# Token-row projections of an encoder block: 512 columns of w_in per matmul instead of 256

## The chip, the cores and the metric

The kernel runs on one core of one Trainium2 chip. The core has five engines that each work through their own instructions in order and wait for one another by semaphores: TensorE (matmuls, PE in the profile, with its weight loads as PEld), VectorE (DVE), ScalarE (ACT), GpSimd (POOL) and SyncE (SP), which here issues nearly all DMAs. The metric is the device time of one execution in microseconds, lower is better.

## What is computed

The reference is one layer of an encoder block on 1024 tokens of 1024 channels, in float32: an input norm with a modulation, two token mixers on the same normed input `h` (bidirectional retention with 4 heads of 128, differential attention with 4 heads), a gated merge, an output projection, and 16 expert feed-forwards of which each takes 128 tokens. What matters here is the projection of `h` and what its columns are used for:

```
h = _rmsnorm(x, norm_mix_g[l]) * (1.0 + sc1) + sh1
proj = h @ w_in[l]
rq, rk, rv, rg, dq1, dq2, dk1, dk2, dvv, gr, gd = jnp.split(proj, split_points, axis=-1)
rq = _rotate(rq.reshape(B, S, RET_HEADS, RET_DK), pos)
rk = _rotate(rk.reshape(B, S, RET_HEADS, RET_DK), pos) * (RET_DK ** -0.5)
...
```

`rq`, `rk`, `rv`, `rg` (retention) and `dvv` (the values of the attention) have 512 columns each, and these five are wanted with tokens as rows. `dq1` to `dk2` and the gates `gr`, `gd` are wanted with channels as rows.

## The kernel before

**Split numbers.** A float32 product is made of three matmuls on rounded parts: every operand is kept as a high part (`hi`, rounded by ScalarE) and a low part (`lo`, the difference, by VectorE or GpSimd). `mm3` issues high x high, high x low, low x high. `hH` and `hL` hold the parts of `h`, with channels as rows, in eight pieces of 128 channels (`k`).

**Weights.** The class `Weights` walks through one list of row blocks of 128 x 1024 float32 (512 KB). The first 44 are `w_in`: blocks 0 to 7 for the attention's q and k, then five groups of four for `dvv`, `rv`, `rk`, `rq`, `rg` (called v, r_v, r_k, r_q, r_g here), then 16 for the gates. `load` issues a block's DMA on SP's queue into one of two buffers `raw`; `split_to` makes `hi` (ScalarE) and `lo` (GpSimd in this stage, as `W.eng = G`) in one of four buffer pairs (`HL = 4`); `take` hands blocks to a projection. A raw buffer is refilled after its `lo`; the refill is issued three ticks after the split (`W.lazy = 3`), and a tick passes with each step of the weave.

**Two kinds of projection.** `proj_T` makes 128 channels as rows: one block, 8 steps, moving operand `h` with 512 columns, the weights held in the array. `proj_N` makes tokens as rows: 128 tokens of `hH`/`hL` are held in the array and the weights move. In before.py one call makes 256 columns from two blocks (each block has four `k` side by side, 256 columns each), in 16 steps of 12 matmuls with 256 columns. Its sums stand in a PSUM tile `mm` [128, 2, 256] for 256 tokens, from a pool of two. When a tile is done, `finish`, which runs at the first step of the next tile, issues its evacuation: for v a split in `hi` and `lo` with two stores to `vs` (`evac_v`), for r_v and r_g a copy by ScalarE, for r_k and r_q the rotation, four VectorE operations on 256 columns (`px` x cos, `px` x sin, for two groups of tokens) and two GpSimd operations, and one store to `rs` (`evac_r`). Stores are issued two ticks later on SP's queue.

**The weave.** `weave` runs the steps of the projections (`gen_d`: five `proj_T`, then v and r_v; `gen_r`: r_k, r_q, r_g; `gen_g`: the gates) and puts steps of side work between them in a fixed proportion: first `gen_mod` (modulation rows, mostly VectorE), then `gen_attn` (107 pieces to 117 steps), then `gen_ret`. This order is the program order on every engine. A round of the attention (128 queries of one head) is: 8 score matmuls into two tiles `big`; on VectorE the bias with a maximum (`soft`); on ScalarE two exponentials; the scale of the one by ScalarE and the scale-and-add of both by VectorE (`combine`); and, in the next round, 8 transposes and the splits of the result into `at`, with 24 matmuls of probabilities times values every second round.

These lines set how many blocks are held and when the next are split:

```
HL = 4
hl2 = W.take(2, ahead=False)
if t2 < 2 and u == 1 and g == 0:
    W.split_to(W.held + 3 + t2)
```

The last two lines split, in the first and the second of four tiles, the two blocks of the next call.

Of the kernel before, what the change touches and what calls it, by code (L numbers as in the profile page):

```python
# [10 lines left out]
F32 = mybir.dt.float32  # L11
F32R = mybir.dt.float32r
# [64 lines left out]
def lay_out(w):  # L77

    w_in = np.asarray(w["w_in"])[0]
    rq, rk, rv, rg, q1, q2, k1, k2, dv, gr, gd = np.split(  # L80
        w_in, np.cumsum([512, 512, 512, 512, 256, 256, 256, 256, 512, 1024, 1024])[:-1], axis=1)

    def pair(a, b):
        return np.concatenate([a.reshape(D, 4, 1, 64), b.reshape(D, 4, 1, 64)], 2).reshape(D, 512)

    def halves(a):
        return a.reshape(D, 4, 64, 2).transpose(0, 1, 3, 2).reshape(D, 512)

    def blocks(a):
        n = a.shape[1] // 128  # L90
        return a.reshape(8, 128, n, 128).transpose(2, 1, 0, 3).reshape(n, 128, 1024)

    def wide(a):
        n = a.shape[1] // 256
        return a.reshape(2, 4, 128, n, 256).transpose(3, 0, 2, 1, 4).reshape(n * 2, 128, 1024)

    win = np.concatenate([blocks(pair(q1, q2)), blocks(pair(k1, k2)), wide(dv),
                          wide(rv), wide(halves(rk)), wide(halves(rq)), wide(rg), blocks(gr), blocks(gd)], 0)
    wr = np.asarray(w["w_ret_out"])[0].reshape(4, 128, 8, 128).transpose(2, 1, 0, 3)
    wd = np.asarray(w["w_diff_out"])[0].reshape(4, 128, 8, 128).transpose(2, 1, 0, 3)  # L100
    wout = np.concatenate([wr, wd], 2).reshape(8, 128, 1024)

    def col(v, n=8):
        return np.asarray(v).reshape(n, 128).T

    cols = np.concatenate([col(w["c"]), col(w["norm_mix_g"]), col(np.asarray(w["b_ada"])[0, 0:1024]),
                           col(np.asarray(w["b_ada"])[0, 1024:2048]), col(w["diff_subln_g"], 1),
                           col(w["norm_ffn_g"]), col(w["final_g"])], 1)
    lam = np.concatenate([np.asarray(w[n]) for n in ("lambda_q1", "lambda_k1", "lambda_q2", "lambda_k2")], 0)
    rows = np.concatenate([np.asarray(w["b_ada"])[0].reshape(6, 1024)[2:], np.asarray(w["norm_ffn_g"])], 0)  # L110
    return {
        "x": np.asarray(w["x"])[0], "w_ada": np.asarray(w["w_ada"])[0], "w_in": win, "w_out": wout,
        "w_o": np.asarray(w["w_o"])[0], "cols": cols, "lam": lam, "rows": rows,
        "gn": np.asarray(w["ret_gn_g"]), "rel_bias": np.asarray(w["rel_bias"]),
        "w_router": np.asarray(w["w_router"])[0].reshape(8, 128, 16).transpose(1, 0, 2).reshape(128, 128),
        "w_gate": np.asarray(w["w_exp_gate"])[0], "w_up": np.asarray(w["w_exp_up"])[0],
        "w_down": np.asarray(w["w_exp_down"])[0],
    }
# [3 lines left out]
def encoder_block(ctx: ExitStack, tc: tile.TileContext, a, out, lim=99, tap=None):  # L122
# [4 lines left out]
    def r32(ap):  # L127
        return ap.bitcast(F32)
# [408 lines left out]
    def finish():  # L537
        while done:
            done.pop(0)()
# [19 lines left out]

    def proj_N(evac):  # L560

        hl2 = W.take(2, ahead=False)
        for t2 in range(4):
            p = pp.tile([128, 2, 256], F32, name="mm")
            for u in range(2):
                s = slice((t2 * 2 + u) * 128, (t2 * 2 + u) * 128 + 128)
                for g in range(2):
                    if u == 0 and g == 0:
                        finish()
                    if t2 < 2 and u == 1 and g == 0:  # L570
                        W.split_to(W.held + 3 + t2)
                    for k in range(g * 4, g * 4 + 4):
                        hi, lo = hl2[g]
                        c = slice((k % 4) * 256, (k % 4) * 256 + 256)
                        mm3(p[:, u, :], hH[:, k, s], hL[:, k, s], hi[:, c], lo[:, c], k == 0, k == 7)
                    if u and g:
                        done.append(lambda p=p, t2=t2: evac(p, t2))
                    yield

    def evac_qk(i):  # L580
        f = 0.125 if i < 4 else 1.0
# [12 lines left out]
            defer(2, st)  # L594
        return go

    def evac_v(c):
        def go(p, t2):
            oh_ = evp.tile([128, 2, 256], F32R, name="ev0")
            ol_ = evp.tile([128, 2, 256], F32R, name="ev1")  # L600
            split(oh_[:], ol_[:], p[:])

            def st():
                for l, o in ((0, oh_), (1, ol_)):
                    SY.dma_start(r32(vs[l, t2 * 256:(t2 + 1) * 256, c * 256:(c + 1) * 256])
                                 .rearrange("(t p) c -> p t c", p=128), r32(o[:]))
            defer(2, st)
        return go

    tiles = {}  # L610

    def evac_r(n, c):
        def go(p, t2):
            o = evp.tile([128, 2, 256], F32, name="ev0")
            if n in "vg":
                A.activation(o[:], p[:], AF.Copy)
            else:
                f = KSCALE if n == "k" else 1.0
                t1 = evp.tile([128, 2, 2, 2, 64], F32, name="ev1")
                for u in range(2):  # L620
                    t = t2 * 2 + u
                    px = p[:, u, :].rearrange("p (h d) -> p h d", h=4)
                    cb = tiles["cst"][:, t, None, 0:64].to_broadcast([128, 4, 64])
                    sb = tiles["cst"][:, t, None, 64:128].to_broadcast([128, 4, 64])
                    V.scalar_tensor_tensor(o[:, u, :].rearrange("p (h d) -> p h d", h=4), px, f, cb,
                                           op0=OP.mult, op1=OP.mult)
                    V.scalar_tensor_tensor(t1[:, u].rearrange("p h f d -> p (h f) d"), px, f, sb,
                                           op0=OP.mult, op1=OP.mult)
                ox = o[:].rearrange("p u (h f d) -> p (u h) f d", h=2, f=2)
                tx = t1[:].rearrange("p u h f d -> p (u h) f d")  # L630
                G.tensor_tensor(ox[:, :, 0], ox[:, :, 0], tx[:, :, 1], op=OP.subtract)
                G.tensor_tensor(ox[:, :, 1], ox[:, :, 1], tx[:, :, 0], op=OP.add)
            defer(2, lambda: SY.dma_start(rs[n][t2 * 256:(t2 + 1) * 256, c * 256:(c + 1) * 256]
                                          .rearrange("(t p) c -> p t c", p=128), o[:]))
        return go

    def gen_d():
# [7 lines left out]
            defer(3 + 3 * i, lambda i=i: SY.dma_start(r32(qs[i]).rearrange("l p c -> p l c"), xT[:, 2 * i:2 * i + 2, :]))  # L645
        for i in range(3, 8):
            yield from proj_T(evac_qk(i))
        for c in range(2):
            yield from proj_N(evac_v(c))
        for c in range(2):  # L650
            yield from proj_N(evac_r("v", c))

    def gen_mod():

# [195 lines left out]

    def gen_r():
        for n in "kqg":
            for c in range(2):
                yield from proj_N(evac_r(n, c))


    rctx = ctx.enter_context(ExitStack())
# [1105 lines left out]
```

## Time and profile before

| | |
|---|---|
| median of 3 runs | 1611.27 us (1608.58 to 1614.94) |
| the profiled execution, its own time | 1607.37 us |
| its span | 1605.5 us |
| TensorE busy | 1530.6 us, 95% |
| VectorE, ScalarE, GpSimd busy | 1186.8, 886.5, 468.8 us |

The span is the time from the first to the last instruction in the trace; some 2 us of the execution lie around it. Busy time counts an engine's instructions once where they overlap. Matmuls overlap: the mean duration of one is longer than the distance to the next. The projections with tokens as rows run from about 135 to 520 us.

### The profile page before, as it was taken

How to read it: one execution, taken by the hardware profiler on the slowest of the kernel's cores; microseconds unless marked ns; L12 is line 12 of the kernel's file. 1: busy time of each engine (PE TensorE's matmuls, PEld its weight loads, DVE VectorE, ACT ScalarE, POOL GpSimd, SP SyncE). 2: the span in 40 equal slices, each digit the busy share in tenths (PEclk: the TensorE clock that was granted, in tenths of full speed). 3: DMA queues.
4: the chain of work that ended last, by engine and by line, in shares of the span. 5: the costliest groups of instructions: out<-in, count | busy, mean ns of one | idle time of the engine just before them, and what ended most of it. 6: DMA issues, size and time to landing. Idle time of an engine off the chain costs nothing. (4 is left out here: it accounts for less than half of the span.)

```text
span 1605.5 us, 23860 instructions
## 1 busy us (share of the span) xinstructions
PE 1530.6 (95%) x8493; PEld 1282.6 (80%) x8493; DVE 1186.8 (74%) x2037; ACT 886.5 (55%) x1165; POOL 468.8 (29%) x330
## 2 busy tenths in 40 slices
PE   6999999999999999999998997999999999999994
PEld 5778989989898688888877875578888888888882
DVE  6754357778772356663578866899999999999995
ACT  7712156555564444443244343477777777777874
POOL 1342212231311343443000005353433444334310
PEclk8999999999999999999999999999999999999998
DMA  9798453343423484344897687699999999999926
GB/s 315 232 358 305 146 156 113 94 119 100 137 86 105 153 302 149 129 141 145 258 355 242 201 326 267 264 386 397 390 384 392 381 375 387 390 393 386 383 94 249
DMA packets 174019, 408.91 MB, mean 255 GB/s; under 512 B 18712, under 2 KB 71576, under 8 KB 173900
## 3 DMA queue, kind: packets, MB, share of 16 engines
q1 hardware_dynamic: 161916, 368.06, 63.7%
q0 software_dynamic: 9104, 34.08, 7.3%
q10 hardware_dynamic: 2880, 5.24, 0.9%
q8 instruction: 67, 1.10, 0.3%
q14 instruction: 52, 0.43, 0.1%
HBM read 350.65 MB, written 57.73 MB: 254 GB/s over the span
## 5 line engine op out<-in xcount | busy, mean ns | idle before, releaser
L131 PE MATMUL big<-hi,xh 128*128 128x512 f32 x494 | 202.1, 409 | 1.7 <-DVE yraw L1800 1.7
L131 PE MATMUL big<-lo,xh 128*128 128x512 f32 x494 | 195.5, 396 | 0.0
L131 PE MATMUL big<-hi,xl 128*128 128x512 f32 x494 | 195.5, 396 | 0.0
L140 POOL TENSOR_TENSOR lo<-raw,hi 128x1024 fp32r<-128x1024 f32 x44 | 107.4, 2442 | 280.1 <-ACT hi L139 275.8
L140 DVE TENSOR_TENSOR lo<-eraw,hi 128x1024 fp32r<-128x1024 f32 x139 | 169.4, 1226 | 23.9 <-ACT hi L139 20.3
L131 PE MATMUL mm<-hi,hH 128*128 128x256 f32 x640 | 183.8, 287 | 0.0
L131 PE MATMUL mm<-lo,hH 128*128 128x256 f32 x640 | 180.9, 283 | 0.0
L131 PE MATMUL mm<-hi,hL 128*128 128x256 f32 x640 | 180.8, 282 | 0.0
L139 ACT ACTIVATE hi<-eraw 128x1024 fp32r<-128x1024 f32 x139 | 146.0, 1057 | 40.4 <-PE big L131 39.9
L1615 POOL TENSOR_SCALAR oh<-tab,aff 128x128 bf16<-128x128 f32 x112 | 157.1, 1426 | 2.6 <-DVE aff L1736 2.6
L131 PE MATMUL mm<-hH,hi 128*128 128x512 f32 x352 | 141.7, 402 | 3.4 <-ACT hH L415 2.3
L131 PE MATMUL mm<-hL,hi 128*128 128x512 f32 x352 | 138.1, 392 | 1.6 <-DVE hL L420 1.6
L131 PE MATMUL mm<-hH,lo 128*128 128x512 f32 x352 | 137.9, 392 | 0.0
L131 PEld LDWEIGHTS mm<-hi,hH 128*128 128x128 f32 x640 | 122.2, 191 | 4.8 <-DVE xt L678 1.7
L131 PEld LDWEIGHTS mm<-lo,hH 128*128 128x128 f32 x640 | 122.4, 191 | 1.3
L131 PEld LDWEIGHTS mm<-hi,hL 128*128 128x128 f32 x640 | 122.3, 191 | 0.0
L783 ACT ACTIVATE e<-e,m 128x1024 f32<-128x1024 f32 x64 | 73.6, 1150 | 82.8 <-DVE m L777 82.7
L131 PEld LDWEIGHTS big<-hi,xh 128*128 128x128 f32 x494 | 93.3, 189 | 23.4 <-ACT hi L139 2.1
L131 PEld LDWEIGHTS big<-hi,xl 128*128 128x128 f32 x494 | 92.9, 188 | 22.5 <-DVE xl L140 0.3
L131 PEld LDWEIGHTS big<-lo,xh 128*128 128x128 f32 x494 | 93.1, 189 | 21.1 <-issue 1.2
L139 ACT ACTIVATE hi<-raw 128x1024 fp32r<-128x1024 f32 x79 | 83.0, 1055 | 35.9 <-PE big L131 10.6
L775 DVE CUSTOM_DVE_ANT_0 e<-big,strip 128x1024 f32<-128x1024 f32 x64 | 77.8, 1216 | 30.6 <-PE big L131 30.6
(491 smaller groups left out, 3791.1 us busy)
## 6 DMA issues: line engine op xcount, KB each, us to landing
raw<-in_w_in_dram SPq DMA_DIRECT2D x43, 512.0 KB
eraw<-in_w_gate_dram SPq DMA_DIRECT2D x41, 512.0 KB
eraw<-in_w_up_dram SPq DMA_DIRECT2D x38, 512.0 KB
eraw<-in_w_down_dram SPq DMA_DIRECT2D x34, 512.0 KB
wada<-in_w_ada_dram POOLq DMA_DIRECT2D x16, 1024.0 KB, 8.5
eraw<-in_w_o_dram SPq DMA_DIRECT2D x26, 512.0 KB
mh<-in_w_gate_dram SPq DMA_DIRECT2D x17, 512.0 KB
wada<-in_w_ada_dram SPq DMA_DIRECT2D x16, 512.0 KB
```

The lines of the kernel that those rows point to most:

```text
L131: T.matmul(o, l, r, start=start, stop=stop)
L139: A.activation(hi, src, AF.Copy)
L140: eng.tensor_tensor(lo, src, r32(hi), op=OP.subtract)
L775: V.tensor_tensor_reduce(e[:], p[:], strip[:, 896 - 128 * qb:1920 - 128 * qb], scale=1.0, scalar=-3.0e38, op0=OP.add, op1=OP.max, accum_ou ...
L783: A.activation(e[:], e[:], AF.Exp, bias=m[:], accum_out=z[:])
L1615: eng.tensor_scalar(o[:, g], tab[:, C_IOTA:C_IOTA + 128], slots[e][:, g:g + 1], None, op0=OP.is_equal)
```

## The change

The host lays out the five groups of `w_in` in another way (`wide`): a block has two `k` with all 512 columns each instead of four `k` with 256. One call of `proj_N` makes all 512 columns from four blocks in 32 steps of 6 matmuls with 512 columns, for eight tiles of 128 tokens; five calls take the place of ten. The PSUM tile is [128, 512], as large as before, an evacuation has 128 tokens x 512 columns, and a store is 128 rows of 512 contiguous columns. The next call's blocks are split in the last of the eight tiles, after the first, second and third step, and the rest at the next `take`.

```
     def wide(a):
-        n = a.shape[1] // 256
-        return a.reshape(2, 4, 128, n, 256).transpose(3, 0, 2, 1, 4).reshape(n * 2, 128, 1024)
+        return a.reshape(4, 2, 128, 512).transpose(0, 2, 1, 3).reshape(4, 128, 1024)
...
     def proj_N(evac):
-        hl2 = W.take(2, ahead=False)
-        for t2 in range(4):
-            p = pp.tile([128, 2, 256], F32, name="mm")
-            for u in range(2):
-                s = slice((t2 * 2 + u) * 128, (t2 * 2 + u) * 128 + 128)
-                for g in range(2):
-                    if u == 0 and g == 0:
-                        finish()
-                    if t2 < 2 and u == 1 and g == 0:
-                        W.split_to(W.held + 3 + t2)
-                    for k in range(g * 4, g * 4 + 4):
-                        hi, lo = hl2[g]
-                        c = slice((k % 4) * 256, (k % 4) * 256 + 256)
-                        mm3(p[:, u, :], hH[:, k, s], hL[:, k, s], hi[:, c], lo[:, c], k == 0, k == 7)
-                    if u and g:
-                        done.append(lambda p=p, t2=t2: evac(p, t2))
-                    yield
+        hl4 = W.take(4, ahead=False)
+        for t in range(8):
+            p = pp.tile([128, 512], F32, name="mm")
+            r = slice(t * 128, t * 128 + 128)
+            for g in range(4):
+                if g == 0:
+                    finish()
+                hi, lo = hl4[g]
+                for u in range(2):
+                    k, c = g * 2 + u, slice(u * 512, u * 512 + 512)
+                    mm3(p[:], hH[:, k, r], hL[:, k, r], hi[:, c], lo[:, c], k == 0, k == 7)
+                if g == 3:
+                    done.append(lambda p=p, t=t: evac(p, t))
+                if t == 7 and g < 3:
+                    W.split_to(W.held + 5 + g)
+                yield
...
-                    SY.dma_start(r32(vs[l, t2 * 256:(t2 + 1) * 256, c * 256:(c + 1) * 256])
-                                 .rearrange("(t p) c -> p t c", p=128), r32(o[:]))
+                    SY.dma_start(r32(vs[l, t * 128:(t + 1) * 128, :]), r32(o[:]))
...
-                for u in range(2):
-                    t = t2 * 2 + u
-                    px = p[:, u, :].rearrange("p (h d) -> p h d", h=4)
...
+                px = p[:].rearrange("p (h d) -> p h d", h=8)
+                cb = tiles["cst"][:, t, None, 0:64].to_broadcast([128, 8, 64])
+                sb = tiles["cst"][:, t, None, 64:128].to_broadcast([128, 8, 64])
+                V.scalar_tensor_tensor(o[:].rearrange("p (h d) -> p h d", h=8), px, f, cb, op0=OP.mult, op1=OP.mult)
+                V.scalar_tensor_tensor(t1[:].rearrange("p h f d -> p (h f) d"), px, f, sb, op0=OP.mult, op1=OP.mult)
...
-        for c in range(2):
-            yield from proj_N(evac_v(c))
-        for c in range(2):
-            yield from proj_N(evac_r("v", c))
+        yield from proj_N(evac_v())
+        yield from proj_N(evac_r("v"))
```

ScalarE where v ends and r_v begins, before. `hi` is the high part of a weight block, `ev0` an evacuated tile (line 139 for v, line 616 for r_v).

```order
L139 ACTIVATE ev0_1548<-mm_1490 128x512
L139 ACTIVATE ev0_1605<-mm_1547 128x512
L139 ACTIVATE hi_1635<-raw_1418 128x1024
L616 ACTIVATE ev0_1672<-mm_1604 128x512
L139 ACTIVATE hi_1699<-raw_1488 128x1024
L616 ACTIVATE ev0_1760<-mm_1671 128x512
```

The same place in the changed kernel (line 138 for v and `hi`, line 613 for r_v).

```order
L138 ACTIVATE ev0_1335<-mm_1301 128x512
L138 ACTIVATE ev0_1368<-mm_1334 128x512
L138 ACTIVATE hi_1378<-raw_1142 128x1024
L138 ACTIVATE hi_1392<-raw_1144 128x1024
L138 ACTIVATE hi_1406<-raw_1396 128x1024
L138 ACTIVATE hi_1418<-raw_1398 128x1024
L138 ACTIVATE ev0_1423<-mm_1367 128x512
L613 ACTIVATE ev0_1462<-mm_1422 128x512
```

The four blocks of r_v now stand in a row, ahead of the evacuation of v's last tile; before, blocks came one at a time between evacuations.

ScalarE under the attention, at the end of r_v, before: `e,z` is an exponential, `at0` the high part of a turned tile, `e<-e,r` the scale of `combine`, `y` the result of probabilities times values.

```order
L783 ACTIVATE e_2449,z_2469<-e_2449,m_2450 128x1024
L139 ACTIVATE hi_2483<-raw_2017 128x1024
L794 ACTIVATE e_2445<-e_2445,r_2499 128x1024
L819 ACTIVATE y_2531<-t_2506 128x256
L783 ACTIVATE e_2558,z_2566<-e_2558,m_2559 128x1024
L139 ACTIVATE at0_2568<-t_2572 128x4x128
```

The changed kernel where r_v ends and r_k begins.

```order
L138 ACTIVATE hi_1960<-raw_1416 128x1024
L772 ACTIVATE e_1966,z_1974<-e_1966,m_1967 128x1024
L138 ACTIVATE at0_1976<-t_1980 128x4x128
L138 ACTIVATE at0_1978<-t_1987 128x4x128
L772 ACTIVATE e_1970,z_1994<-e_1970,m_1971 128x1024
L138 ACTIVATE hi_2002<-raw_1433 128x1024
L138 ACTIVATE hi_2016<-raw_2006 128x1024
L783 ACTIVATE e_1966<-e_1966,r_2028 128x1024
L138 ACTIVATE hi_2051<-raw_2008 128x1024
L613 ACTIVATE ev0_2056<-mm_1951 128x512
L772 ACTIVATE e_2065,z_2073<-e_2065,m_2066 128x1024
```

All four blocks of r_k are split within one and a half rounds of the attention; two come ahead of the scale of `combine`, and the fourth ahead of the next exponential.

SP's queue where v ends and r_v begins, in the changed kernel: `raw` is a weight block, `vs` a store of v.

```order
L603 DMA vs<-ev_1368 128x512
L603 DMA vs<-ev_1369 128x512
L254 DMA raw<-in_w_in_dram 128x1024 x4
L603 DMA vs<-ev_1423 128x512
L603 DMA vs<-ev_1424 128x512
L625 DMA rs_v<-ev_1462 128x512
```

The loads of four blocks now follow one another; before, a load stood alone between the stores of four tiles or two.

## Rows read from the trace of the kernel before

**Rows 1.** The page: span, and busy time of TensorE and its weight loads.
```profile
span 1605.5 us, 23860 instructions
PE 1530.6 (95%) x8493; PEld 1282.6 (80%) x8493; DVE 1186.8 (74%) x2037; ACT 886.5 (55%) x1165; POOL 468.8 (29%) x330
```

**Rows 2.** Busy time by stretch: length, busy per engine (count), granted clock, DMA share, GB/s.
```profile
141.00:187.00 46.00, 46.00 (x373) 44.31 (x372) 21.69 (x22) 8.16 (x12) 11.08 (x6) 1.00 0.61 207
...
256.00:494.00 238.00, 231.05 (x1743) 219.97 (x1742) 180.65 (x375) 133.93 (x211) 58.12 (x49) 1.00 0.37 108
```

**Rows 3.** Timeline of TensorE in v, start and length: first and last of 66.
```profile
149.75 0.28 PE L131 MATMUL mm<-hi,hH 128*128 128x256 f32 x1
...
157.55 0.28 PE L131 MATMUL mm<-hi,hL 128*128 128x256 f32 x1
```

**Rows 4.** The same in the last `proj_T`: first and last of 12, then of 15.
```profile
125.77 0.39 PE L131 MATMUL mm<-hH,hi 128*128 128x512 f32 x1
...
128.26 0.39 PE L131 MATMUL mm<-hH,lo 128*128 128x512 f32 x1
...
131.20 0.40 PE L131 MATMUL mm<-hH,hi 128*128 128x512 f32 x1
...
134.41 0.39 PE L131 MATMUL mm<-hH,lo 128*128 128x512 f32 x1
```

**Rows 5.** The page's groups: a third of the token-row matmuls, busy and mean ns.
```profile
L131 PE MATMUL mm<-hi,hH 128*128 128x256 f32 x640 | 183.8, 287 | 0.0
```

**Rows 6.** Timeline: a weight block's split and the load into its raw buffer.
```profile
158.36 1.05 ACT L139 ACTIVATE hi<-raw 128x1024 fp32r<-128x1024 f32 x1
...
159.50 2.39 POOL L140 TENSOR_TENSOR lo<-raw,hi 128x1024 fp32r<-128x1024 f32 x1 [8.27 <-ACT hi L139]
...
161.92 0.35 SPq L255 DMA_DIRECT2D raw<-in_w_in_dram  x1
```

**Rows 7.** DMA traffic from 161 to 171 us, in 40 slices of 0.25 us.
```profile
DMA  0004995076799930000000003999997000000093
GB/s 0 0 0 168 348 352 180 0 164 213 311 475 377 426 131 33 0 0 0 0 0 0 0 0 127 356 299 357 352 348 254 4 0 0 0 0 0 0 180 98
```

**Rows 8.** Timeline of ScalarE, VectorE and GpSimd, a round of the attention in r_k.
```profile
262.63 2.40 POOL L140 TENSOR_TENSOR lo<-raw,hi 128x1024 fp32r<-128x1024 f32 x1 [28.49 <-ACT hi L139]
263.62 2.49 DVE L795 SCALAR_TENSOR_TENSOR e<-e,r 128x1024 f32<-128x1024 f32 x1 [1.63 <-ACT e L794]
...
266.48 1.23 DVE L775 CUSTOM_DVE_ANT_0 e<-big,strip 128x1024 f32<-128x1024 f32 x1 [0.37 <-PE big L131]
...
267.94 1.15 ACT L783 ACTIVATE e<-e,m 128x1024 f32<-128x1024 f32 x1 [2.00 <-DVE m L777]
...
269.27 1.10 ACT L139 ACTIVATE at<-t 128x512 fp32r<-128x512 f32 x2
...
271.11 0.41 DVE L625 SCALAR_TENSOR_TENSOR ev<-mm,cst 128x256 f32<-128x256 f32 x1
...
272.68 1.15 ACT L794 ACTIVATE e<-e,r 128x1024 f32<-128x1024 f32 x1 [1.18 <-DVE r L790]
...
273.86 1.29 DVE L795 SCALAR_TENSOR_TENSOR e<-e,r 128x1024 f32<-128x1024 f32 x1 [0.52 <-ACT e L794]
...
275.07 1.22 DVE L775 CUSTOM_DVE_ANT_0 e<-big,strip 128x1024 f32<-128x1024 f32 x1
```

**Rows 9.** Timeline of TensorE: the scores and the transposes of one round.
```profile
265.36 2.02 PE L131 MATMUL big<-kt,qt 128*128 128x512 f32 x8
...
379.92 1.03 PE L807 MATMUL t<-idt,e 128*128 128x128 f32 x8
```

**Rows 10.** Waits from 112 to 520 us (total, times, longest), then a stretch as in rows 2.
```profile
PE big L131 <- DMA qt<-qs: 3.3, 1, 3.3
...
PE t L807 <- DVE e L795: 1.9, 5, 0.5
...
204.00:208.00 4.00, 2.58 (x13) 2.13 (x14) 1.12 (x1) 0.00 (x0) 0.00 (x0) 1.00 1.14 293
```

More of the change, by code (lines that the diff above doesn't have):

```diff
@@ L595, in evac_qk, with evac_v, go @@
         return go
[L597 to L600, printed above, removed]
+    def evac_v():
+        def go(p, t):
+            oh_ = evp.tile([128, 512], F32R, name="ev0")
+            ol_ = evp.tile([128, 512], F32R, name="ev1")
             split(oh_[:], ol_[:], p[:])
@@ L610, in encoder_block, with evac_r, go @@
     tiles = {}
-    def evac_r(n, c):
-        def go(p, t2):
-            o = evp.tile([128, 2, 256], F32, name="ev0")
+    def evac_r(n):
+        def go(p, t):
+            o = evp.tile([128, 512], F32, name="ev0")
             if n in "vg":
@@ L618, in go @@
                 f = KSCALE if n == "k" else 1.0
-                t1 = evp.tile([128, 2, 2, 2, 64], F32, name="ev1")
-                for u in range(2):
-                    t = t2 * 2 + u
-                    px = p[:, u, :].rearrange("p (h d) -> p h d", h=4)
[L623 to L634, printed above, removed]
+                t1 = evp.tile([128, 4, 2, 64], F32, name="ev1")
+                px = p[:].rearrange("p (h d) -> p h d", h=8)
[3 more added lines that the diff above has]
+                V.scalar_tensor_tensor(t1[:].rearrange("p h f d -> p (h f) d"), px, f, sb, op0=OP.mult, op1=OP.mult)
+                ox = o[:].rearrange("p (h f d) -> p h f d", h=4, f=2)
+                G.tensor_tensor(ox[:, :, 0], ox[:, :, 0], t1[:, :, 1], op=OP.subtract)
+                G.tensor_tensor(ox[:, :, 1], ox[:, :, 1], t1[:, :, 0], op=OP.add)
+            defer(2, lambda: SY.dma_start(rs[n][t * 128:(t + 1) * 128, :], o[:]))
         return go
@@ L852, in gen_r @@
         for n in "kqg":
-            for c in range(2):
-                yield from proj_N(evac_r(n, c))
+            yield from proj_N(evac_r(n))
     rctx = ctx.enter_context(ExitStack())
```

## The prediction

> **What bounds the kernel now.** I read the page's shares first: TensorE is busy for 95% of the span [rows 1], so a change to its instruction stream can show in the end time. Then the table by stretch: the projections with tokens as rows ("N calls" below) run from about 135 to 520 us. Where nothing but small side work is woven in, from 141 to 187 us, TensorE is busy 46.00 of 46.00 us and no other engine reaches half of that; under the attention, from 256 to 494 us, TensorE has 231.1 of 238.0, VectorE 180.7, ScalarE 133.9 [rows 2]. TensorE sets the pace in both, with little room in the second.
>
> Next, what one matmul costs. The page gives 287 ns for a matmul with 256 columns [rows 5], but that is its length from start to end, and the next one starts before it ends. The timeline has the real price, from start to start: 66 matmuls of 256 columns from 149.75 to 157.55 us, 65 intervals, are 0.120 us each [rows 3]. With 512 columns, 11 intervals from 125.77 to 128.26 and 14 from 131.20 to 134.41, together 5.70 us over 25, are 0.228 us each; the two runs alone give 0.226 and 0.229 [rows 4]. Two of 256 columns cost 0.240, one of 512 costs 0.228: the difference is 0.012 us, far from the half that the number of instructions suggests.
>
> **What is removed.** Ten calls of 16 steps become five of 32, so the count of steps, 160, and the side work woven between them stay. A step was 12 matmuls of 256 columns, 1.44 us, and is 6 of 512, 1.37 us. 160 x 0.072 = 11.5 us come off TensorE (10.3 and 13.1 by the two runs apart). I take 11.5.
>
> The Trainium skill ("TensorE: Matmul & The Clock Gate", Back-to-back issue gap) gives N/2.4 + 2.5 ns per matmul at full clock: 109.2 ns for 256 columns, 215.8 for 512. By that the saving would be an estimated 2.5 us instead of 11.5. Rows 3 and 4 disagree with it at both widths; the measurement decides.
>
> **Evacuation and stores.** An evacuation still reads 512 columns every four steps. The rotation of k and q takes two VectorE operations of 512 columns instead of four of 256, 0.41 us each [rows 8]: between 0.8 us, if the columns cost nothing, and the 1.6 of before, so up to 0.8 less per tile, on an engine that doesn't pace the stage. GpSimd's two keep their size, the stores are as many and as large, in longer rows. All this I cost at nothing: it lies beside TensorE, and its buffers come round only every two tiles (over 10 us).
>
> **What is added: the four blocks come at once.** There are four pairs of hi/lo buffers and two of raw. Before, a call held two blocks, and the next two were split into free buffers during its first half. Now a call holds all four, so block 1 of the next call can be split only when TensorE has read this call's block 1 for the last time, in the last tile; call that moment T0. A split is ScalarE's hi, 1.05 us, then GpSimd's lo, 2.39 us, and its raw buffer is refilled when lo ends: 3.53 us from hi's start to the issue at 161.92 [rows 6]. That load's traffic runs until slice 16 of 0.25 us, 165.0 us: 3.1 us from issue to landing [rows 7]. So blocks 3 and 4 can't be in raw before blocks 1 and 2 are through.
>
> *v to r_v, no attention:* block 1 is done 3.6 us after T0, block 2 at 6.0 (GpSimd takes them one behind the other). Block 3: buffer free 3.6, landed 6.7, hi 7.8, lo 10.2. Block 4: free 6.0, landed 9.1, hi 10.2, lo 12.6. TensorE has three steps left, until 4.1, and runs the new call's step 1 until 5.5, step 2 from 6.0 to 7.4, step 3 from 10.2 to 11.6, step 4 from 12.6 to 14.0. Without waits it would end at 9.6: **4.4 us** lost.
>
> *Under attention* more work of TensorE lies between: 8 transposes 1.0 us and 8 score matmuls 1.8 (at 0.228; 2.02 with the last one's full length) [rows 9], 24 of probabilities times values 2.9 (at 0.120). But ScalarE is in order, and behind a hi that waits for its raw stand the exponentials, the scale of `combine` and the splits of `at`; VectorE's scale-and-add, next in the chain, takes 1.29 us alone and 2.49 beside a lo on GpSimd [rows 8].
>
> *r_v to r_k:* TensorE is due, after T0, at the transposes at 8.3, at the values at 12.0. ScalarE: hi to 1.2, exponential, two `at`, exponential to 4.9, hi of block 2 to 6.0, of block 3 to 7.8, scale to 8.9; VectorE's scale-and-add ends at 10.2, or 11.4 doubled, so the transposes wait up to 3.1. Block 2's lo ends at 8.4, block 4 lands at 11.5, hi 12.6, evacuation 13.2, exponential 14.4, first `at` 15.0 and its low half 15.7: the values start at 15.7 instead of 12.0. **3.7 us.** The new call's step 4 (due 16.8, then 20) finds lo, ready at 15.0.
>
> *r_k to r_q:* values and scores precede the second step of the last tile, so hi of block 2 waits for 6.1; scale follows hi of block 3, 12.1 to 13.2, the doubled scale-and-add ends at 15.7, transposes due at 14.1: **1.6 us**. *r_q to r_g:* hi of block 4 ends at 13.4, scale 14.5, scale-and-add 17.0, transposes due at 14.4: **2.6 us**.
>
> *Into the first N call and out of the last:* nothing. The projections around them need one block per eight steps; the one late block of the first is ready 3.6 us after its buffer comes free and is due after three steps, 4.1. Were that cover gone, it would cost what a split exceeds it by, about 1 us.
>
> On SP's queue the refills come in a row ahead of the stores and of the query tiles; the row's third load waits for block 3's lo (10 to 11 us), the queries behind it are due some 10 us later. I cost that at nothing.
>
> **Sum.** The profiled execution took 1607.4 us; -11.5 +4.4 +3.7 +1.6 +2.6 = +0.8, so 1608.2. It lies 3.9 below the median of the runs, 1611.3; on the median's scale the forecast is **1612**. A measurement here tells about 0.5%, 8 us, from no change, so this is "same".
>
> Bounds. The three waits under attention lie between 0 (TensorE's own work covers all) and one whole round of the ScalarE-VectorE chain each, 8.6 us from 266.48 to 275.07 [rows 8]; nearest is the working above, since each duration in it has its row. The first lies between 4.0 (a landing of 2.7) and 6 (stores in front of the load). A gain from the waits is excluded: nothing is fetched earlier than before.
>
> **Rivals.**
> 1. *Faster: the attention covers its three refills.* Then -11.5 +4.4 = -7.1, 1604; with the better end of both, -13.1 +4.0, 1602. For it: a round of TensorE's own work lasts some 9 us, a refill 3, and TensorE hardly ever waited for the scale-and-add before, 1.9 us in 5 times [rows 10]. Against: ScalarE's order, which no work of TensorE changes.
> 2. *Slower: the refill lands late.* Landing time enters the first wait once and stands ahead of ScalarE's queue in the others. At 5 us instead of 3.1 each of four handovers is 1.9 longer: +0.8 +7.6 = +8.4, the point from which it counts as slower; at 6 us +12, 1624. For it: SP issues the loads in order, beside stores and the next head's keys. Against: 3.1 us was measured with other traffic in front.
> 3. *Slower: attention paces its stage.* A round of the attention is three of its 107 pieces to 117 steps, so 3.28 steps: with scores, transposes and values 4.7 + 1.8 + 1.0 + 1.4 = 9.0 us before and 8.7 after; the chain's 8.6 is hardly shorter. If it binds, 117 of 160 steps save nothing: +0.8 +8.4, 1621. Against: TensorE was busy for 97% of that stretch, and some rounds of the chain have no rotation in them.
> 4. *Slower: half as many matmuls save nothing*, since a matmul's time goes by its columns alone: the waits of 12.3 us stay, 1624. Rows 3 and 4 speak against it: a pair of 256 columns is 0.012 us longer than one of 512. The Trainium skill's formula above comes near this case (an estimated 1621).
>
> A longer wait might also lower TensorE's clock. Around its 3.3 us wait for queries at 202 to 205 us the granted clock stayed 1.00, the 2.4 GHz level, and no wait above is longer, so I add nothing [rows 10].
>
> **How the numbers follow.** Forecast case 0.62; rival 1 0.19, of which 0.16 falls beyond 0.5%; rival 2 0.10, rival 3 0.07, rival 4 0.02. Faster 0.16, same 0.64, slower 0.20. The range takes rival 1's better end and rivals 3 and 4: 1602 to 1622.
>
> **What would show it.** 960 matmuls of 512 columns 0.226 to 0.230 apart show the gain; 0.216 or 0.240 refutes it. After v, three gaps on TensorE that end with GpSimd's lo, the longest near 2.8 us; at the attention's three handovers, TensorE waiting for `e` or `at`, 2 to 4 us each, with ScalarE idle ahead of a hi until its raw lands. If those gaps are missing, rival 1 is right; if raw lands 5 us after issue, rival 2; if TensorE waits for the scale-and-add all through the attention, rival 3. The forecast is wrong if the waits total under 4 or over 20 us.

## The result, and the profile after

The changed kernel takes 1634.07 us (median of 4 runs, 1629.77 to 1636.31) against 1611.55 us for the kernel before on the same chip (1608.58 to 1614.94). The ratio is 1.0141, with an interval from 1.012 to 1.0162: 22.5 us slower, where 1612 was forecast with a range up to 1622. Repeated on another chip the ratio was 1.0122 (1.0102 to 1.0142).

The page of the kernel after, the lines that answer to [rows 1]:

```profile
span 1627.7 us, 21905 instructions
...
PE 1533.0 (94%) x7533; PEld 1238.5 (76%) x7533; DVE 1183.1 (73%) x2005; ACT 887.1 (55%) x1165; POOL 466.6 (29%) x330
```

TensorE issues 960 matmuls fewer and is busy 2.4 us longer. The waits tell more. Those of TensorE from 112 to 590 us in the kernel after (in total, times, longest):

```profile
PE big L130 <- DMA kt<-ks: 9.8, 3, 8.3
PE t L796 <- DVE e L784: 9.0, 3, 4.6
PE t L130 <- ACT lq L876: 6.9, 6, 3.1
PE mm L130 <- POOL lo L139: 3.5, 4, 1.9
PE big L130 <- DMA qt<-qs: 2.2, 1, 2.2
PE big L130 <- DVE vdl L139: 2.1, 2, 1.2
PE mm L130 <- ACT hi L138: 1.0, 1, 1.0
```

They add up to 34.5 us. In the kernel before the same stretch has the two waits of [rows 10], 3.3 and 1.9, and these:

```profile
PE big L131 <- DMA kt<-ks: 4.5, 5, 1.9
PE big L131 <- DVE vdl L140: 3.6, 4, 1.2
...
PE t L131 <- ACT lq L888: 1.8, 3, 0.9
PE t L131 <- DVE at L140: 1.1, 1, 1.1
```

That is 16.2 us, so waits grew by 18.3 us. The forecast had 12.3 in all, and two things that it cost at nothing stand here: the keys (`kt`) with 8.3 us at one place, and `lq`, tiles that the side work behind the attention loads, with 6.9.

The second thing is the clock. The table by stretch of the kernel after; behind the busy times of the five engines stands TensorE's granted clock (1.00 is 2.4 GHz; 0.50 would be 1.2 GHz all through):

```profile
180.00:200.00 20.00, 15.98 (x50) 9.01 (x49) 2.05 (x3) 3.19 (x4) 7.79 (x4) 0.83 0.47 145
...
260.00:280.00 20.00, 16.27 (x85) 13.86 (x84) 10.91 (x21) 11.07 (x17) 8.66 (x5) 0.91 0.62 183
...
360.00:380.00 20.00, 18.73 (x90) 15.56 (x91) 10.14 (x21) 7.21 (x13) 2.58 (x4) 0.84 0.59 150
...
520.00:540.00 20.00, 15.78 (x55) 9.87 (x54) 1.12 (x3) 7.45 (x11) 7.08 (x3) 0.93 0.50 157
```

The kernel before has 1.00 in every microsecond from 60 to 620 us. In the kernel after the clock fell at 189, 209, 267, 356, 458 and 537 us, each time in or just behind one of the waits above. Taken in stretches of 1 us from 112 to 620 us, what is missing to 1.00 adds up to 15.4 us; counted only while TensorE is busy, where alone it costs time, to 12.2 us.

**Where the 22 us lie.** I compare the two traces at the same instructions of the program: TensorE's score matmuls under the attention, ScalarE's evacuations before and behind it. "Lost" is by how much the distance between the two grows at a handover:

| handover | forecast | lost | waits of TensorE there, less those of before | low clock while busy |
|---|---|---|---|---|
| v to r_v | 4.4 | 6.6 | 4.0 | 3.1 |
| r_v to r_k | 3.7 | 5.4 | 3.7 | 1.7 |
| r_k to r_q | 1.6 | 8.8 | 9.1 - 2.3 | 2.7 |
| r_q to r_g | 2.6 | 6.2 | 4.6 | 1.6 |
| r_g to the gates | 0 | 6.7 | 6.9 - 1.8 | 1.7 |
| sum | 12.3 | 33.7 | 24.2 | 10.8 |

Between the handovers the kernel after wins back 12 us, and from the gates on (550 us) it stays 21.6 us behind. The last two columns add up to 35.0, 1.3 more than was lost; steps inside these stretches save too. A balance by kinds, from 112 to 590 us: waits +18.3, clock +12.2, and -9.7 for the width (worked out with the first experiment) give +20.8.

The handovers in the trace. *v to r_v*, TensorE in the kernel after:

```profile
183.12 0.50 PE L130 MATMUL mm<-lo,hH 128*128 128x512 f32 x1 [0.38 <-POOL lo L139]
...
185.54 0.50 PE L130 MATMUL mm<-hi,hH 128*128 128x512 f32 x1 [0.99 <-ACT hi L138]
187.97 0.50 PE L130 MATMUL mm<-lo,hH 128*128 128x512 f32 x1 [1.92 <-POOL lo L139]
...
190.71 0.79 PE L130 MATMUL mm<-lo,hH 128*128 128x512 f32 x1 [0.72 <-POOL lo L139]
191.30 0.63 PE L130 MATMUL mm<-hi,hL 128*128 128x512 f32 x1
191.72 0.63 PE L130 MATMUL mm<-hi,hH 128*128 128x512 f32 x1
192.15 0.63 PE L130 MATMUL mm<-lo,hH 128*128 128x512 f32 x1
```

The gaps are where they were forecast, at each block of the new call, 4.0 us together. The clock fell at 189 us, behind the third. From then on the matmuls start 0.42 to 0.43 us apart instead of 0.23, and each is 0.63 long instead of 0.39: the same work at half the clock. The Trainium skill ("TensorE: Matmul & The Clock Gate", Part 1, "Wait — 56ns, not 53.3ns?") gives N divided by 1.2 GHz for matmuls on the slow clock, 426.7 ns for 512 columns, and the rows agree.

*r_v to r_k*, three engines of the kernel after:

```profile
262.51 1.06 ACT L138 ACTIVATE hi<-raw 128x1024 fp32r<-128x1024 f32 x1 [1.90 <-DMA raw<-in_w_in_dram]
...
264.64 2.43 DVE L784 SCALAR_TENSOR_TENSOR e<-e,r 128x1024 f32<-128x1024 f32 x1 [4.58 <-ACT e L783]
...
267.22 1.18 PE L796 MATMUL t<-idt,e 128*128 128x128 f32 x6 [3.73 <-DVE e L784]
```

This is the forecast chain: a hi waits for its raw, the scale stands behind it, the scale-and-add takes 2.43 beside a lo, and the transposes wait 3.73 us, for which up to 3.1 was forecast. The forecast's 3.7 stood one step further on, at the values, and there TensorE doesn't wait. The clock came on top.

*r_k to r_q*, TensorE and SP in the kernel before:

```profile
338.09 2.02 PE L131 MATMUL big<-kt,qt 128*128 128x512 f32 x8
...
339.78 2.41 SPq L726 DMA_DIRECT2D kt<-ks  x4
...
348.74 1.16 PE L131 MATMUL big<-kt,qt 128*128 128x512 f32 x4 [1.92 <-DMA kt<-ks]
```

The same in the kernel after:

```profile
345.16 2.01 PE L130 MATMUL big<-kt,qt 128*128 128x512 f32 x8
...
348.80 3.75 SPq L254 DMA_DIRECT2D raw<-in_w_in_dram  x2
...
353.54 2.40 SPq L715 DMA_DIRECT2D kt<-ks  x4
...
360.47 2.04 PE L130 MATMUL big<-kt,qt 128*128 128x512 f32 x4 [8.28 <-DMA kt<-ks]
363.32 2.05 PE L130 MATMUL big<-kt,qt 128*128 128x512 f32 x4 [0.81 <-DMA kt<-ks]
```

In the kernel before the next head's keys are issued at 339.78 us, while the head's last scores (338.09) still run, and TensorE waits 2.3 us for them (0.4 and 1.9). After, the last scores begin at 345.16, but the keys stand on SP's queue behind two refills, the second of which waits for a lo until 352.2. They go out at 353.54, and the first scores that use them start 6.9 us later.

*r_g to the gates*, SP and TensorE in the kernel after:

```profile
527.32 0.42 SPq L866 DMA_DIRECT2D lq<-yds  x1
531.02 7.45 SPq L254 DMA_DIRECT2D raw<-in_w_in_dram  x3
...
538.90 0.33 SPq L866 DMA_DIRECT2D lq<-yds  x1
...
536.20 1.02 PE L130 MATMUL t<-lq,ones 128*1 128x512 f32 x2 [3.13 <-ACT lq L876]
...
543.59 1.02 PE L130 MATMUL t<-lq,ones 128*1 128x512 f32 x2 [1.81 <-ACT lq L876]
```

The same in small: three refills take SP from 531.02 to 538.47, and a load of `lq`, which TensorE's side work needs every few steps, stands behind them; the second wait, 1.81 us, is for it. The 3.13 us of the first wait have another cause: `lq` was there, but its square on ScalarE stood behind a hi that waited 3.9 us for its raw.

### The profile page after: what moved, and what is told of

Same layout as the page of the kernel before. It is cut to its first block, busy times and chain, and to the rows that moved or that the text cites. A ratio compares the mean times of both kernels' runs of the same rounds, so it can differ in the third digit from the quotient of the medians.

```text
span 1627.7 us, 21905 instructions
## 1 busy us (share of the span) xinstructions
PE 1533.0 (94%) x7533; PEld 1238.5 (76%) x7533; DVE 1183.1 (73%) x2005; ACT 887.1 (55%) x1165; POOL 466.6 (29%) x330
## 5 line engine op out<-in xcount | busy, mean ns | idle before, releaser
L130 PE MATMUL mm<-hi,hH 128*128 128x512 f32 x320 | 130.3, 407 | 1.0 <-ACT hi L138 1.0
L130 PE MATMUL mm<-lo,hH 128*128 128x512 f32 x320 | 126.6, 396 | 3.5 <-POOL lo L139 3.5
L130 PE MATMUL mm<-hi,hL 128*128 128x512 f32 x320 | 126.9, 397 | 0.0
L130 PEld LDWEIGHTS big<-lo,xh 128*128 128x128 f32 x494 | 93.3, 189 | 21.1 <-issue 1.2
L130 PE MATMUL big<-hi,ah 128*128 128x512 f32 x244 | 96.8, 397 | 0.0
L130 PE MATMUL big<-hi,al 128*128 128x512 f32 x244 | 95.2, 390 | 0.0
L130 PE MATMUL big<-lo,ah 128*128 128x512 f32 x244 | 95.0, 389 | 0.0
```

Of the source, the lines that this page charges most:

```text
L130: T.matmul(o, l, r, start=start, stop=stop)
```

## Experiments

Ratios are to the kernel before on the same chip. A profiled execution can differ from another of the same kernel by some us: the changed kernel, taken twice, lay 21.8 and 25.0 us behind the kernel before at 745 us. Smaller differences than that are not read. The traced execution of the kernel before took 1607.4 us, and its medians are 1611 to 1615, so a distance to its trace can come out some us too long; times and ratios go by the medians.

**The changed kernel again (e0_after).**

> The changed kernel again, beside the kernel before on one chip. If its loss is that of its program and not of a chip, the ratio is 1.012 to 1.016, and TensorE's granted clock again falls in stretches of some 3.5 us each right after its longer waits between 180 and 560 us, some 15 us of full clock in sum; if the low stretches were chance, they are elsewhere or missing.

1632.28 us against 1613.47: 1.0122 (1.0102 to 1.0142). Low clock at 189 to 197, 268 to 272, 357 to 368, 456 to 463 and 538 to 549 us, 17.1 us of clock missing instead of 15.4, at the same handovers; the stretch at 209 is missing, though TensorE waited 2.1 us for queries there as well (2.2 in the first trace). The loss belongs to the program.

**The width alone undone (e1_cols256).**

```
-   mm3(p[:], hH[:, k, r], hL[:, k, r], hi[:, c], lo[:, c], k == 0, k == 7)
+   for v in range(2):
+       cv = slice(u * 512 + v * 256, u * 512 + v * 256 + 256)
+       mm3(p[:, v * 256:v * 256 + 256], hH[:, k, r], hL[:, k, r], hi[:, cv], lo[:, cv], k == 0 and v == 0, k == 7 and v == 1)
```

> The changed kernel with each matmul of 512 columns issued as two of 256, in the same order of blocks, steps, tiles, stores and splits: only the width of the instruction is undone. Theory (a pair of 256 columns costs 0.012 us more than one of 512, and the handovers cost what they cost whatever the width): 160 steps x 0.072 = 11.5 us more than the changed kernel, 1645 us, 1.021 of the time before. Rival (half as many matmuls save nothing, or an estimated 2.5 us by the formula of the Trainium skill, page TensorE: Matmul & The Clock Gate, section Back-to-back issue gap): 1634 to 1637, 1.014 to 1.016.

1634.76 us against 1615.37: 1.0125 (1.0108 to 1.0141). This is what the rival said, not the theory. But the rival's reason is not in the trace. Two steps under the attention, with 24 matmuls of 256 columns, in this kernel (first matmul, and what follows the last):

```profile
225.50 0.28 PE L130 MATMUL mm<-hi,hH 128*128 128x256 f32 x1
...
228.38 1.03 PE L798 MATMUL t<-idt,e 128*128 128x128 f32 x8
```

and two with 12 of 512 columns in the kernel after:

```profile
226.07 0.39 PE L130 MATMUL mm<-hi,hH 128*128 128x512 f32 x1
...
228.84 1.04 PE L796 MATMUL t<-idt,e 128*128 128x128 f32 x8
```

2.88 against 2.77 us: a step saves 0.055 us here. Without attention 24 steps of v took 34.71 us instead of 36.55, 0.077 a step. With 43 steps of the second kind and 117 of the first that is 9.7 us of TensorE's work, a little less than the 11.5 of the sum. What reached the end is at most 3.4 us (25.2 behind the kernel before at 745 us, against 21.8 and 25.0 for the changed kernel). The narrow kernel waits less: TensorE's waits from 112 to 590 us are 31.1 instead of 34.5 us, and 8.2 us of clock are missing while it is busy instead of 12.2. A TensorE that arrives sooner at a handover whose end is set by loads and ScalarE waits longer: the evacuation behind those 24 steps starts at 178.94 us in the narrow kernel and at 175.75 in the changed one, r_v's last evacuation at 267.60 and 267.72, so nothing of the lead is left.

**Keys and lq on ScalarE's queue (e2_actq).**

```
-   SY.dma_start(r32(kt[l * 64:l * 64 + 64, :]), r32(ks[h, l, s * 64:s * 64 + 64, :]))
+   (A if h else SY).dma_start(r32(kt[l * 64:l * 64 + 64, :]), r32(ks[h, l, s * 64:s * 64 + 64, :]))
...
-   SY.dma_start(y[:], yds[h, :, c])
+   A.dma_start(y[:], yds[h, :, c])
```

> The changed kernel, with the attention's loads of keys (kt, four for each later head) and the loads of lq after r_g issued from ScalarE's queue instead of SP's, at the same places of the program; the weights' loads stay on SP. Theory (at r_k to r_q and r_g to the gates, TensorE waits because these loads stand on SP's queue behind refills that wait for a lo): TensorE's wait for kt falls from 8.3 us to under 3, its waits for lq from 6.9 us in all to under 2, the time falls by 8 to 11 us to 1623 to 1626. Rival (ScalarE stands at a hi that waits for its raw, whatever SP does): the waits move to transposes and lq, the time stays within 3 us of 1634.

1634.79 us against 1615.37: 1.0117 (1.0097 to 1.0137), so no gain that can be told, where 8 to 11 us were expected. The waits moved: at r_k to r_q 3.3 us for keys instead of 8.3, for `lq` 5.1 in all instead of 6.9, at r_g to the gates 2.7 us lost instead of 6.7; but one head earlier the keys, now behind an exponential on ScalarE, made a wait of 2.4 us where it was 0.7. Another engine's queue is no free place either. This did not decide it; the move on SP's own queue below did.

**First and last tiles in pairs (e3_pairs).**

```
+   order = [(t, g) for g in range(4) for t in range(2)]
+   order += [(t, g) for t in range(2, 6) for g in range(4)]
+   order += [(t, g) for g in range(4) for t in range(6, 8)]
...
```

> The changed kernel with 512 columns, but the first two and the last two tiles of a call run block by block as pairs (tile 0 and 1 with block 1, both with block 2, and so on; tiles 2 to 5 as they are; tiles 6 and 7 again by blocks), so that block 1 comes free six steps before the end of a call instead of three, the splits are two steps apart, and block 4 of the next call is wanted after six steps instead of three. Theory (the loss is the refill chain of hi, lo, load, hi, lo in too little time): v to r_v loses under 1 us instead of 6.6, ScalarE's waits for raw fall from 19 us to under 8 from 112 to 560 us, each of the other handovers loses 3 us less; 1612 to 1620. Rival (the loss is the order on SP's and ScalarE's queues, which stays): 1626 or more, with the wait for kt above 5 us.

1634.7 us against 1615.37: 1.0124 (1.0107 to 1.0141). ScalarE's waits for raw fell from 19.1 to 5.1 us, the longest for keys is 2.1 us. TensorE's waits from 112 to 560 us are 34 us all the same, by other names:

```profile
PE t L130 <- ACT lq L881: 10.4, 4, 6.4
...
PE big L130 <- DMA kt<-ks: 4.7, 3, 2.1
PE mm L130 <- DVE ev L626: 4.0, 2, 2.5
PE mm L130 <- DVE ev L139: 3.1, 2, 1.5
```

A pair takes both `mm` tiles at once, so a new pair waits for the evacuation of the last (`mm` after `ev`). At r_g to the gates 11.5 us are lost instead of 6.7: the longest wait for `lq`, 6.4 us, is SP's order again, since that load goes out at 521.31 us behind a refill that waits for a lo until 520.77. The first theory misses its time. The rival has the time, not the wait for keys above 5 us: the refill chain can be loosened, but the order in pairs pays for it in PSUM and on SP's queue.

**Splits of blocks 3 and 4 later (e5_late).**

```
-   hl4 = W.take(4, ahead=False)
+   W.held = W.taken
+   W.split_to(W.held + 2)
+   hl4 = [W.hl.pop(W.taken + i) for i in range(2)]
+   W.taken += 2
...
+   if t == 0 and g < 2:
+       W.split_to(W.held + 3 + g)
+       hl4.append(W.hl.pop(W.taken))
+       W.taken += 1
-   if t == 7 and g < 3:
+   if t == 7 and g < 2:
```

> The changed kernel with the splits of blocks 3 and 4 of a call issued later, after the first and second step of that call instead of in the last tile and at the call's start, so that ScalarE does not stand at a hi that waits for its raw ahead of the attention's exponentials and scales. Theory (ScalarE's order makes the waits under attention): the waits for e at the transposes, 9.0 us in 3 times, fall to under 3, TensorE's waits for lo grow by 1 to 3 us; 1626 to 1630. Rival (the refill chain itself sets when TensorE goes on): what leaves the transposes comes back at mm after lo, and the time is 1632 to 1640.

1631.01 us against 1615.37: 1.009 (1.007 to 1.0109), the best of the kernels with five calls of 512 columns so far. The transposes' waits fell from 9.0 to 2.0 us, as ScalarE's order would have it; TensorE's waits for lo grew from 3.5 to 7.9, more than the 1 to 3 of the theory; the wait for keys at r_k to r_q stayed, 7.8 us. At r_g to the gates, where fewer refills now stand in a row, 1.8 us are lost instead of 6.7.

**The handover's low parts on VectorE (e8_lov).**

```
+   W.held = W.taken
+   W.split_to(W.held + 4, V if W.held > 8 else None)
...
-   W.split_to(W.held + 5 + g)
+   W.split_to(W.held + 5 + g, V)
```

> The changed kernel with the low parts of the blocks that are split at a handover made by VectorE (1.23 us each where it makes them elsewhere in the kernel) instead of GpSimd (2.4 us). Theory (the chain hi, lo, load, hi, lo is what TensorE waits for): v to r_v loses 3 to 4 us instead of 6.6, the refills are issued 1 to 2 us sooner at the others, 1620 to 1627, 1.006 to 1.010. Rival (under attention VectorE's own chain and the queues' order decide): only v to r_v gains, the transposes wait as long or longer, 1630 or more, 1.012 or above.

1638.07 us against 1613.47: 1.0158 (1.0141 to 1.0176). v to r_v lost 4.8 us instead of 6.6; under the attention the waits for `e` grew to 9.8 us in 3 times, and keys cost 6.3. The rival was right: a shorter chain of one step is worth little where VectorE's own work and the queues' order end last.

**Three calls, or two (e7_three, e7_two).** The kernel before, with `proj_N` and the layout of the weights chosen for each of the five groups: `proj_N4` is the changed kernel's `proj_N`, `d` stands for v. A call of 512 columns that follows two of 256 finds two of its blocks split already. `WIDE` is "dkg" in the one kernel and "dq" in the other.

```
+   if n in WIDE:
+       yield from proj_N4(evac_v4() if n == "d" else evac_r4(n), 3 if nxt else 2)
+   else:
+       for c in range(2):
+           yield from proj_N(evac_v(c) if n == "d" else evac_r(n, c), nxt and c == 1)
```

> 512 columns in three calls only: v, r_k and r_g hold four blocks, r_v and r_q run as before in two calls of 256 columns that hold two, so that no call with four blocks follows another. Theory (the loss belongs to a handover between two calls that both hold all four buffers): ScalarE waits less than 6 us for raw, at most one stretch of low clock, TensorE's waits from 112 to 560 us within 5 us of the kernel before; 96 steps save 0.05 to 0.074 us each, some 5.5 us, so 0.995 to 1.002 of the time before. Rival (the calls with 512 columns cost something by themselves, in evacuation, stores or TensorE): at least 1.006.

> 512 columns in two calls only, v and r_q; r_v, r_k and r_g run as before. Theory as for the kernel with three such calls: 64 steps save some 4.0 us, the four changes between kinds of call cost under 1 us each: 0.996 to 1.001 of the time before, and r_g's end is as before (no lq behind refills). Rival: a change between kinds costs 3 us or more, 1.005 or above.

Two calls: 1606.97 us against 1613.47, 0.9958 (0.9939 to 0.9976). Three: 1627.46, 1.0099 (1.0082 to 1.0116). Both have no 512-column call behind another, and ScalarE waits under 3 us for raw in either, so the theory that the loss belongs to such neighbours alone falls with the kernel of three. The waits of the kernel with three calls, from 112 to 560 us:

```profile
PE big L134 <- DMA kt<-ks: 9.3, 4, 7.6
PE t L134 <- ACT lq L950: 5.3, 5, 3.0
```

and of that with two:

```profile
PE big L134 <- DMA kt<-ks: 3.6, 4, 1.4
PE big L134 <- DMA qt<-qs: 3.6, 1, 3.6
...
PE t L134 <- ACT lq L950: 1.7, 3, 0.8
```

The three calls lose 7 us at the end of r_k and 4.7 at the end of r_g, the two places where a call with four blocks ends just where keys or `lq` are due, and 3 us where r_q hands over to r_g's four blocks (transposes 2.8 us). In the kernel with three calls SP spends 340.92 to 344.65 on two refills, and the keys go out at 345.65; with two they go out at 341.74, ahead of the refills.

**Keys ahead of the refills (e9_ktfirst, e10_three_first).** In the first, the changed kernel with `load_h(h + 1)` moved up:

```
     ps = scores(i)
+    if (q2, b) == (3, 1) and h < 3:
+        load_h(h + 1)
...
-    if (q2, b) == (3, 1) and h < 3:
-        load_h(h + 1)
```

> The changed kernel with one move: the loads of the next head's strip and keys (kt) stand in the program right after the last scores of a head, so that on SP's queue at r_k to r_q they come ahead of the two refills that wait for a lo, and the refills wait behind them. Theory (SP's order makes the wait for kt): TensorE's wait for kt at r_k to r_q falls from 8.3 us to under 3, with it part of the 5 us of low granted clock behind it; 5 to 8 us less than the changed kernel, 1.007 to 1.011 of the time before. Rival (the refills and ScalarE's order set when the round goes on, the wait only changes its name): TensorE waits as long there for e or mm, 1.012 to 1.016.

1627.17 us against 1613.99: 1.0079 (1.0055 to 1.0104). SP and TensorE at r_k to r_q:

```profile
346.88 2.40 SPq L715 DMA_DIRECT2D kt<-ks  x4
349.38 4.25 SPq L254 DMA_DIRECT2D raw<-in_w_in_dram  x2
...
354.96 1.17 PE L130 MATMUL big<-kt,qt 128*128 128x512 f32 x4 [1.17 <-DMA kt<-ks]
360.68 1.06 PE L796 MATMUL t<-idt,e 128*128 128x128 f32 x8 [3.18 <-DVE e L784]
```

The wait for keys is 1.2 us instead of 8.3, and the low clock there is one short stretch (362 to 366). The refills, now later, make the transposes wait 3.2, so 5 of the 8 us are won. That is SP's order shown by SP's order alone; the other 3 are a wait of the kind that was forecast here (1.6 for the transposes). The other kernel has three calls, the same move, and one split instead of two in r_g's last tile:

> The kernel with three calls of 512 columns (v, r_k, r_g), with keys ahead of the refills as above, and only one block of the gates split in r_g's last tile, so that fewer refills stand ahead of lq. Theory (what made three calls slower than two is only what stands behind refills on SP at the end of r_k and of r_g): the wait for kt falls from 7.6 us to under 2, the waits for lq from 5.3 to under 2.5, 0.995 to 1.001 of the time before. Rival (the end of a call with four blocks costs by itself): above 1.005.

1614.12 us against 1613.99: 1.000 (0.9988 to 1.0012). Waits for keys 1.8 us in all, for `lq` 2.8; the 3 us at r_q to r_g stay. From 1.0099 to 1.000 by the order of instructions alone; in the two traces the distance at 745 us falls by 11 us, from 13.3 to 2.4.

**Such a wait in the kernel before (e11_ktlate).**

```
+    if (q2, b) == (0, 0) and h:
+        load_h(h)
     ps = scores(i)
...
-    if (q2, b) == (3, 1) and h < 3:
-        load_h(h + 1)
```

> The kernel before, all calls with 256 columns, with one move: the loads of strip and keys of heads 1 to 3 are issued behind one store more on SP's queue, some 8 to 10 us later, just ahead of the scores that need them. This makes the one wait that the changed kernel has at r_k to r_q, without 512 columns and without refills. Theory (such a wait costs itself and, behind it, a stretch in which TensorE's clock is granted at 1.2 GHz): three waits for kt of 5 to 9 us, each followed by 3 to 7 us of low granted clock; 17 to 30 us more than before, 1.010 to 1.019. Rival (the low clock in the changed kernel has another cause): the waits come, the granted clock stays at 1.00 and the time grows by the waits alone.

1629.32 us against 1613.99: 1.0101 (1.0078 to 1.0125). TensorE at the first of the three places:

```profile
281.13 2.04 PE L131 MATMUL big<-kt,qt 128*128 128x512 f32 x4 [7.89 <-DMA kt<-ks]
```

The table of the stretch around it, with a granted clock of 0.57:

```profile
276.00:288.00 12.00, 6.59 (x26) 5.35 (x27) 2.77 (x6) 1.24 (x2) 3.60 (x3) 0.57 0.86 205
```

And all waits for keys from 112 to 560 us:

```profile
PE big L131 <- DMA kt<-ks: 18.1, 6, 7.9
```

Waits of 7.9, 2.0 and 7.5 us, each with low clock in it or behind it. At the gates this kernel is 21.1 us behind the kernel before, while its waits for keys grew by 13.6 (18.1 - 4.5). The clock gives the rest: 7.2 us are missing while TensorE is busy around these three waits, and nothing else was changed. So the low clock of the changed kernel needs neither 512 columns nor refills in a row, only the waits. By the medians the kernel is 15.3 us slower, a little under the 17 to 30 of the theory.

**The kernel with two calls once more (e7_two_again).**

> The kernel with two calls of 512 columns (v and r_q) once more, in five rounds: if the first result was the kernel's and not the chip's, the ratio to the kernel before is 0.994 to 0.998 again; with savings by the width alone (24 to 32 steps at 0.07 and 32 at 0.05 us, under 4 us) it would be 0.9975 or above.

1606.03 us against 1613.61: 0.9954 (0.9938 to 0.9969). It beats both kernels, the kernel before by some 7 us, more than the 4 of its width (in the two traces it lies 3.8 and 5.0 us ahead at 745 us). In r_q alone it gains 4.4 us, where 32 steps x 0.055 are 1.8. The waits that the kernel before has in the middle of r_q, 1.1 us for `at` and 0.9 for keys, aren't there. That is the call and not the width: the wait of 1.1 for `at` stands in every kernel that runs r_q in two calls (before, late keys, both with three calls) and in none that runs it in one, the one with matmuls of 256 columns among them, which wins 3.0 us on the kernel before at these two places.

## Why the prediction was wrong

The saving was nearly right; the price was not. Three things put at nothing came to 24 us: the keys behind the refills (7), `lq` behind refills and a hi (5 of wait) and the clock (12).

1. **The saving: right in kind and nearly in size, wrong in what it is worth.** Forecast 0.226 to 0.230 between matmuls of 512 columns; measured 0.227 in v and 0.231 under the attention, so 9.7 us instead of 11.5. The step that failed is that this comes off the end. It comes off only where TensorE ends last, and the five handovers are not such places: at most 3.4 us arrived (first experiment on the width).
2. **v to r_v, 4.4: mechanism right.** Three gaps ending with GpSimd's lo, as said, and one with hi; the waits are 4.0, the longest 1.9 instead of 2.8. A load took 3.7 us from issue (180.75) to hi's start (184.44), where the sum had 3.1 [rows 6, 7]. (From hi's start to the refill's issue at 161.92 it is 3.56 us, not 3.53, which changes nothing.) What lifts the loss to 6.6 is 3.1 us of clock.
3. **r_v to r_k, 3.7: right chain, and some luck in the number**, wrong by the clock's 1.7. The transposes waited 3.73 us instead of up to 3.1, and the values, which were to bring the sum to 3.7, not at all. r_q to r_g: the transposes waited 4.6 instead of 2.6; the order was as told, its durations too short. One of them was left out: a VectorE product of 128x1 in front of the scale-and-add took 2.32 us (454.62 to 456.94) while GpSimd made a lo (454.58 to 456.92), and 0.16 a round later.
4. **r_k to r_q, 1.6: the step that failed outright.** "the row's third load waits for block 3's lo (10 to 11 us), the queries behind it are due some 10 us later. I cost that at nothing." The sentence looked at the queries and at the third load. In the row at r_k to r_q stand the next head's keys too, which the program loads behind the last scores, are due one round later, and already made TensorE wait in the kernel before. They stood behind the second load's lo, and the place lost 8.8 us instead of 1.6. Moving the keys ahead took 5 back; with three calls, together with the move at `lq`, it was 11 in the traces (1.0099 to 1.000 by the medians).
5. **Out of the last call, "nothing": wrong by 6.7.** The gates' blocks were looked at, the side work's `lq` not. It stands on the same two queues: on SP behind refills, on ScalarE behind a hi that waits for its raw.
6. **The clock, "I add nothing": wrong by 12.** The one wait of 3.3 us at 1.00 [rows 10] was taken for a rule, and it was the exception. Of the 14 traces, eleven have a wait of 1.9 to 5.2 us for queries at this place, ahead of the attention's first scores; in nine of them the clock falls in it or just behind it, with 2.2 us in the changed kernel itself and with 3.6 and 3.2 in the two traces of the kernel with two calls. Only the 3.3 us of the kernel before and 2.1 us in the changed kernel's second trace left it at 1.00. So chance has a part in it, and one trace could not tell. The reason given, that no wait would be longer, did not hold in the forecast itself, which had 3.7.
7. **Rivals.** The slower side did come, at 1634 beyond all three rivals on that side. Rival 2 (late landing) is real with 0.6 us for the load after v and explains little. Rival 3 (attention paces) does not hold: from 380 to 440 us TensorE was busy 60.00 of 60.00. Rival 4, 1624, comes nearest with rival 2's far end, but not for its reason: the width does save, 0.055 to 0.077 us a step. The one that was missing is the queue: who stands behind an instruction that waits.

## What to carry to other kernels

When a change makes refills come in a row, list for each handover everything that stands behind them on the issuing queue, and ask of each item when it can be issued and when it is due; "nothing" is an answer only after that list. Price a new wait of TensorE at itself plus the half-speed stretch behind it (here 12 us on 18), and don't take one wait that kept the clock for a rule. Work taken off an engine is worth little if the places where it hands over end with another: try the change at those calls alone whose ends are free, as the two calls here that gain 7 us where five lose 22.

## What the runs showed of the hardware

- In the changed kernel TensorE's clock fell to the 1.2 GHz level in or right after waits of 8.3, 4.6, 3.7, 3.1 and 2.2 us, and after three of 0.4 to 1.9 us between 183 and 188 us. Waits of like length need not do it: 3.3 us for queries in the kernel before and 2.1 us in the changed kernel's second trace left it at 1.00, 1.9 us at the same place in the kernel with late splits did not.
- The next head's four loads of keys (256 KB each), issued over 2.4 us, held TensorE's second half of the scores until 9.8 us after the first issue beside two refills (353.54 to 363.32), until 8.1 us ahead of them (346.88 to 354.96).
- A DMA issued by ScalarE is no way around a queue: it stood behind an exponential there, and TensorE waited 2.4 us for keys where SP's queue had cost 0.7.
- A VectorE product of 128x1 took 2.32 us beside a GpSimd lo that ended with it, and 0.16 us without one.
- Between 790 and 1020 us, where no edit reaches, executions differ by up to 8 us (the distance of one kernel to the kernel before grew from 23.3 to 31.8 us there). What this comes from was not tried.
